# Three modulation vectors on TensorE in column groups, and decay matrices in two interleaved coroutines

## The chip, the cores and the metric

One core of a Trainium2 chip runs the whole program. The metric is device time in microseconds (us), from the first instruction to the last; small is good.

## The reference, cut to what matters

Two transformer blocks run over a sequence of 256 tokens of width 1024, all in float32. The first block is modulated by a condition `c`: eight vectors of 1024 numbers come out of one row times a matrix each.

```python
c_act = jax.nn.silu(c)                                   # (1, 1024)
mod = c_act @ w_ada[l] + b_ada[l]                        # w_ada: 1024 x 6144
sh1, sc1, g1, sh2, sc2, g2 = jnp.split(mod, 6, axis=-1)  # six vectors of 1024
h = modulate(rms_norm(x, norm1_w[l]), sh1, sc1)
mix = hybrid_mixer(h, ...)      # h @ w_in, gated delta rule over 8 heads, short convolution
x = x + g1[:, None, :] * mix
h = modulate(rms_norm(x, norm2_w[l]), sh2, sc2)
x = x + g2[:, None, :] * swiglu(h, ...)
shf, scf = jnp.split(c_act @ w_ada_f + b_ada_f, 2, axis=-1)
```

Inside the mixer each of the 8 heads has a log-decay `g` per token; `decay[c, s] = exp(g_c - g_s)` for `c >= s`, a triangular matrix per head and half of the sequence, weighs the products `k k^T` and `q k^T`. A triangular inverse of `I + beta * (k k^T) * decay` then gives what the heads write. The second block (attention with a position bias, a convolutional FFN) is not touched.

## The kernel before, in words

Activations lie transposed, features on the 128 partitions, 256 tokens along the free axis. A **unit** is one 128-wide column block of a weight matrix times all 256 tokens. Float32 accuracy is had by splitting each weight tile into two float32r halves: ScalarE copies `raw` to `whi`, VectorE subtracts to get `wlo`, and TensorE runs three 128x256 matmuls per 128 rows of the contraction (`whi` times high, `whi` times low, `wlo` times high activations), 24 for a unit of 1024 rows. They write to four PSUM banks `mm0` to `mm3`. Everything else that TensorE does (transposes, the heads' small float32 products) goes to four banks `sd0` to `sd3`.

Weights come in **chunks** of up to 1 MB through a ring of four `raw` buffers (RAW = 4), issued by SyncE in a fixed order. A buffer is given back when its last reader is through. Splits are made up to four units ahead (LAG = 4).

The order of the work is not written out: the program text runs a planner. Coroutines (`gens`) hold the side work (decays, keys, inverses), `postq` the work on a finished unit's PSUM bank; each has an estimated ready time, and `tick()` steps those whose time has come between two triples of matmuls. `account()` holds the planner's prices. What comes out is one fixed order per engine, and each engine works in that order. When the planner has nothing to put in, `pump()` moves its clock on and the engines simply wait.

What the change touches:

- `ada_chunk(v, j)`: one 1 MB chunk holds rows 256j to 256j+255 of the 1024 columns of vector `v`. Three of the vectors, G1, SC2 and SH2, are needed only at the output projection (`post_wo`); their 12 chunks are sprinkled among the units from the short-convolution stage to the projection. VectorE multiplies a 128x1024 half chunk by its column of `cact` and adds it to `acc` (8 operations per vector), and `ada_finish` then transposes `acc` in eight 128x128 pieces on TensorE and sums over the free axis with two reductions.
- `gdn_gates`: makes the gates, then the decay matrices `gD[:, h]` of the 8 heads one after the other: ScalarE scales two masks (`gx`), TensorE makes three products (`sd<-ce,gx` and `sd<-cn,gsums`), ScalarE takes the exponential, GpSimd masks it.
- `gdn_k(h)`: the product `k k^T` of a head (`sd<-KQ`), its norms, and the decayed matrix `AK`. It waits for the key `"D"`, which stands for all 8 heads.
- `small_inverses`: when all 8 `AK` are there, they go through DRAM into another layout, VectorE does a back-substitution of 31 steps (`ct<-KQ,KQ` and `KQ<-KQ,ct`), and the result returns through DRAM (`blk<-KQ`, then `U<-blk`) to be transposed on TensorE (`sd<-cn,U`) by `inverse`.
- `post_z(j)`: the first gate unit takes the buffer that the masks `ce` lie in (tag K).

Of the kernel before, what the change touches and what calls it, by code (L numbers as in the profile page):

```python
# [11 lines left out]
F32 = mybir.dt.float32  # L12
# [32 lines left out]
BK = 32  # L45

C_ID, C_LV = 0, 128
C_GT = C_LV + len(LEVELS) * P
C_LE = C_GT + P
C_ALL = C_LE + P  # L50

# [1 line left out]
def shape_constants():  # L53
    t = np.arange(P)
    c = np.zeros((P, C_ALL), np.float32)
    c[:, C_ID:C_ID + P] = np.eye(P)
    c[:, C_GT:C_GT + P] = 1.0 * (t[:, None] > t[None, :])
    c[:, C_LE:C_LE + P] = 1.0 * (t[:, None] <= t[None, :])
    for i, b in enumerate(LEVELS):
        o = C_LV + i * P  # L60
        c[:, o:o + P] = 1.0 * (((t[:, None] // b) % 2 == 1) & ((t[None, :] // b) == (t[:, None] // b) - 1))
    dist = np.arange(255, -1, -1)
    nf = np.maximum(dist, 1).astype(np.float32)
    large = 16 + (np.log(nf / np.float32(16)) / np.float32(math.log(128 / 16)) * np.float32(16)).astype(np.int32)
    bucket = np.where(dist < 16, dist, np.minimum(large, 31))
    onehot = (bucket[None, ::-1] == np.arange(32)[:, None]).astype(np.float32)
    return c, onehot
# [3 lines left out]
def body(ctx, tc, a, out):  # L71
# [19 lines left out]
    def front():  # L91
        return max(now[0], et["PE"])
# [51 lines left out]
    def timed(fn, dep):  # L144
        save = dict(cur)
        cur.update(dep=dep, end=dep, eng=None, n=0)
        fn()
        r = cur["end"], cur["n"]
        cur.update(save)
        return r  # L150
# [111 lines left out]
    def bank():  # L262
        i = freeb.popleft()
        return i, pss.tile([P, 512], F32, name=f"sd{i}", tag=f"sd{i}", bufs=1)
# [33 lines left out]
    colC = cst.tile([P, P], F32, name="colC")  # L298
    colD = cst.tile([P, P], F32, name="colD")
    cact = cst.tile([P, KT], F32, name="cact")  # L300
    mod = cst.tile([P, 8, KT], F32, name="mod")
    a1 = cst.tile([P, KT], F32, name="a1")
    a2 = cst.tile([P, KT], F32, name="a2")
# [50 lines left out]
    def emit_event():  # L354
        kind, ci, e = events[st["ev"]]
        load_chunks(ci + 1)
        while st["load"] <= ci:
            t, fn = dq.popleft()
            timed(fn, t)
        raw = chunks[ci]["v"]  # L360
        st["ev"] += 1
        last = st["ev"] == len(events) or events[st["ev"]][1] != ci
        if kind == "w":
            u = e
            n, w = u["nk"], u["ncols"]
            hi = splp.tile([P, KT, P], F32R, name="whi", tag="whi")
            lo = splp.tile([P, KT, P], F32R, name="wlo", tag="wlo")
            if not u["tok"]:
                r = raw[:, :, u["off"]:u["off"] + w]
            else:  # L370
                r = raw[:, u["off"]:u["off"] + n]
                hi, lo = (v.rearrange("p (k a) c -> p k (a c)", a=KT // 2) for v in (hi, lo))
            t, _ = timed(lambda: A.activation(hi[:, :n, :w], r, AF.Copy), chunks[ci]["t"])
            u["hi"], u["lo"] = hi, lo

            def low():
                u["rdy"], _ = timed(lambda: V.tensor_tensor(lo[:, :n, :w], r, hi[:, :n, :w].bitcast(F32), OP.subtract), t)
                if last:
                    chunks[ci]["free"] = u["rdy"]
                    load_chunks(len(chunks))  # L380
            lows.append((t, low, u["idx"]))
        else:
            dq.append((chunks[ci]["t"], lambda: e(raw, 0)))

            def second():
                e(raw, 1)
                if last:
                    chunks[ci]["free"] = et["V"]
                    load_chunks(len(chunks))
            dq.append((chunks[ci]["t"], second))  # L390
# [11 lines left out]
    def acc_tile(v):  # L402
        if v == G2:
            accs_["t"] = slot.tile([P, D], F32, name="acc", tag="E")
        return accs_["t"]

    def ada_chunk(v, j):
        src = a["w_ada"][0] if v < 6 else a["w_ada_f"]
        ci = chunk(src, 2 * j, 2, (v if v < 6 else v - 6) * D, D)

        def go(raw, i):
            k = 2 * j + i
            if k == 0:
                if "ada" in state:
                    wait_gens(("mod", state["ada"]))
                state["ada"] = v
                acc = acc_tile(v)
                V.tensor_scalar(acc, raw[:, 0, :], cact[:, 0:1], None, op0=OP.mult)
            else:
                acc = accs_["t"]  # L420
                V.scalar_tensor_tensor(acc, raw[:, i, :], cact[:, k:k + 1], acc, op0=OP.mult, op1=OP.add)
            if k == KT - 1:
                start(ada_finish(v), 9)
        ada_event(ci, go)

    def ada_finish(v):
        acc = accs_["t"]
        for m0 in (0, 4):
            while not len(freeb):
                yield 0  # L430
            i, b = bank()
            for m in range(4):
                PE.transpose(b[:, m * P:(m + 1) * P], acc[:, (m0 + m) * P:(m0 + m + 1) * P], ident)
            yield 1
            V.tensor_reduce(mod[:, v, m0:m0 + 4], b.rearrange("p (m c) -> p m c", c=P), axis=AX.X, op=OP.add)
            freeb.append(i)
        yield 1
        V.tensor_tensor(mod[:, v], mod[:, v], colA[:, v * 8:v * 8 + 8], OP.add)
        if v == SC1:
            V.scalar_tensor_tensor(a1, mod[:, SC1], 1.0, colA[:, 64:72], op0=OP.add, op1=OP.mult)  # L440
        elif v == SC2:
            V.scalar_tensor_tensor(a2, mod[:, SC2], 1.0, colA[:, 72:80], op0=OP.add, op1=OP.mult)
        elif v == SHF:
            V.tensor_tensor(sha, mod[:, SHF], colA[:, 88:96], OP.mult)
        elif v == SCF:
            V.scalar_tensor_tensor(cf, mod[:, SCF], 1.0, colA[:, 80:88], op0=OP.add, op1=OP.mult)
            V.tensor_tensor(cfa, cf, colA[:, 88:96], OP.mult)
        done.add(("mod", v))
        yield
# [75 lines left out]
    def gdn_gates(t):  # L525
# [43 lines left out]
        sums = cst.tile([P, 2, GH], F32, name="gsums")  # L569
        V.tensor_copy(sums.rearrange("p j c -> p (j c)"), b[:, 0:2 * GH])  # L570
        freeb.append(i)
        for h in range(GH):
            yield from space("gx")
            while not len(freeb):
                yield 0
            i, b = bank()
            t = take("gx")
            g2 = t.rearrange("p (t c) -> p t c", c=P)
            for t_ in range(2):
                A.activation(g2[:, t_], gt, AF.Copy, scale=gg[:, t_, h:h + 1])  # L580
            yield
            PE.matmul(b[:, 0:P], g2[:, 0], le, start=True, stop=True)
            PE.transpose(b[:, P:2 * P], sums[:, 1, h:h + 1].to_broadcast([P, P]), ident)
            PE.matmul(b[:, 2 * P:3 * P], g2[:, 1], le, start=True, stop=True)
            give(t)
            yield
            b3, d3 = (v.rearrange("p (k c) -> p k c", c=P)[:, 0:3:2] for v in (b[:, 0:384], gD[:, h]))
            A.activation(d3, b3, AF.Exp)
            A.activation(gD[:, h, P:2 * P], b[:, P:2 * P], AF.Exp, bias=sums[:, 0, h:h + 1])
            freeb.append(i)  # L590
            yield
            G.tensor_tensor(d3, d3, le[:, None, :].to_broadcast([P, 2, P]), OP.mult)
            yield
        done.add("D")


    ctiles, sct = {}, {}
# [118 lines left out]
    def post_z(j):  # L716
        def f(ps, rel):
            if j == 0:
                zg["z"] = slot.tile([P, KT, S], F32, name="zT", tag="K")
            A.activation(zg["z"][:, j], ps[:, :S], AF.Silu)  # L720
            rel()
            done.add(("z", j))
            yield
        return f
# [21 lines left out]
        V.scalar_tensor_tensor(second, b[:, 256:384], wsc[:, h, 1:2], gD[:, h, 256:384], op0=OP.mult, op1=OP.mult)  # L746

    def gdn_k(h):
        while not len(freeb) or "D" not in done:
            yield 0  # L750
        if "AK" not in state:
            state["AK"] = slot.tile([P, 3, GH, P], F32, name="AK", tag="AK")
# [352 lines left out]

    def post_wo(j):
        def f(ps, rel):
            V.scalar_tensor_tensor(xT[:, j], ps[:, :S], mod[:, G1, j:j + 1], xT[:, j], op0=OP.mult, op1=OP.add)
            rel()
            if j == 0:  # L1110
                next_alloc(h2, "h2h", "h2l", "HI", W2)
                ext_cols(h2["h"], mod[:, SH2])
            yield
            yield from next_input(h2, (j,), a2, "h2")
            if j == KT - 1:
                start(rms_rows(rows2, "rms2"), 3)
                start(normed(h2n, ("L", "AK"), "rms2", "h2n", a2, rows2, mod[:, SH2]))
        return f
# [110 lines left out]
    def post_ffn_out(j0):  # L1229
        def f(ps, rel):  # L1230
            if j0 == 0:
                next_alloc(xa, "xah", "xal", "HI", W2)
                ext_cols(xa["h"], sha)
            for o in range(2):
# [411 lines left out]
    V.tensor_copy(colA[:, 64:72], b[:, 64:72])  # L1646
    freeb.append(i)
    A.activation(cact, colA[:, 104:112], AF.Silu)

    accs_["t"] = slot.tile([P, D], F32, name="acc", tag="E")  # L1650
    ac4 = accs_["t"].rearrange("p (b v c) -> p b v c", v=2, c=P)
# [328 lines left out]
```

## Time and profile before

| | before |
|---|---|
| time, median of 3 runs | 880.76 us (879.03 to 881.55) |
| profiled execution, its own time | 880.34 us |
| its span, first to last instruction | 878.6 us |
| mean granted TensorE clock | 0.99 |
| TensorE busy / VectorE busy | 843.0 us (96%) / 695.6 us (79%) |
| ScalarE busy / GpSimd busy | 498.6 us (57%) / 70.6 us (8%) |

Busy shares are means over stages. A busy TensorE here means that matmuls overlap without a gap: one 128x256 matmul is shown with about 0.28 us, but the next starts about 0.115 us after it, so the pitch from start to start and not the shown duration is the cost of one. PE is TensorE, DVE VectorE, ACT ScalarE, POOL GpSimd, SPq the queue in which SyncE issues transfers. Nearly every operation stands under one line, that of the helper `call`, so the rows are told apart by tile names.

### The profile page before, as it was taken

To read this page: it belongs to the slowest core of one execution; us is meant where nothing else is said; L and a number is where in the kernel's file an instruction comes from. 1 tells how busy PE (TensorE), PEld (TensorE's weight loads), DVE (VectorE), ACT (ScalarE), POOL (GpSimd) and SP (SyncE) were. 2 spreads that over 40 slices of the span, in tenths; PEclk is the share of its full clock that TensorE was granted. 3 is DMA by queue.
4 is the path that set the end of the run, shared out by engine and by line. 5 is a ranking of instruction groups with operands and counts; after the bars stand their busy time and mean duration, and the time that the engine had idled before them with its cause. 6 is when DMAs were issued, how large, how long until landed. Compare 5 with 4: busy or idle time off the path is not lost.

```text
span 878.6 us, 17104 instructions
## 1 busy us (share of the span) xinstructions
PE 843.0 (96%) x6847; PEld 815.1 (93%) x6847; DVE 695.6 (79%) x1314; ACT 498.6 (57%) x902; POOL 70.6 (8%) x83
## 2 busy tenths in 40 slices
PE   6999999997999999999999999999999989999995
PEld 6999899997999999999999999998889989999884
DVE  5899998799858889989877555788758888988452
ACT  3359664455656655575455443567666746777341
POOL 3100023000001200200000011200004000000000
PEclk9999999999999999999999999999999989999998
DMA  9995892656814787758988585652435365555521
GB/s 293 309 300 182 271 300 97 168 193 188 267 61 149 229 281 244 253 180 286 339 284 289 171 276 180 197 188 97 135 107 179 112 214 193 191 171 192 193 71 48
DMA packets 158063, 177.35 MB, mean 202 GB/s; under 512 B 9052, under 2 KB 143584, under 8 KB 157984
## 3 DMA queue, kind: packets, MB, share of 16 engines
q1 hardware_dynamic: 156000, 172.57, 60.7%
q0 software_dynamic: 1472, 3.06, 1.1%
q8 instruction: 54, 0.88, 0.4%
q10 hardware_dynamic: 512, 0.62, 0.2%
q14 instruction: 25, 0.20, 0.1%
HBM read 174.64 MB, written 1.60 MB: 201 GB/s over the span
## 4 chain that ended last, share of the span: by engine, by line
PE 57%; issue 21%; DVE 12%; ACT 6%; DMA 2%; SPq 1%; POOL 1%; POOLq 0%; ACTq 0%; DVEq 0%
PE mm L136 49%; PE sd L136 9%; DVE wlo L136 4%; ACT whi L136 2%; DVE cv L136 2%; DVE acc L136 1%; DMA xtok<-in_x_dram 1%; DMA raw<-in_w_in_dram 1%; SPq L136 1%; DVE ct L136 1%; DMA U<-blk 1%; DVE sct L136 0%; ACT L136 0%; DMA blk<-KQ 0%; ACT KQ L136 0%
## 5 line engine op out<-in xcount | busy, mean ns | idle before, releaser
L136 DVE TENSOR_TENSOR wlo<-raw,whi 128x1024 fp32r<-128x1024 f32 (+2 forms) x267 | 320.1, 1206 | 84.2 <-ACT whi L136 81.0
L136 ACT ACTIVATE whi<-raw 128x1024 fp32r<-128x1024 f32 (+2 forms) x267 | 273.5, 1033 | 145.8 <-PE mm L136 122.7
L136 PE MATMUL mm<-h1h,whi 128*128 128x256 f32 x552 | 160.1, 293 | 0.5 <-ACT h1h L136 0.4
L136 PE MATMUL mm<-h1h,wlo 128*128 128x256 f32 x552 | 153.7, 281 | 2.5 <-DVE wlo L136 2.5
L136 PE MATMUL mm<-h1l,whi 128*128 128x256 f32 x552 | 154.1, 281 | 0.5 <-DVE h1l L136 0.3
L136 PEld LDWEIGHTS mm<-h1h,wlo 128*128 128x128 f32 x552 | 103.9, 189 | 3.1 <-DVE wlo L136 2.9
L136 PEld LDWEIGHTS mm<-h1h,whi 128*128 128x128 f32 x552 | 104.5, 191 | 1.8 <-ACT h1h L136 1.2
L136 PEld LDWEIGHTS mm<-h1l,whi 128*128 128x128 f32 x552 | 103.9, 189 | 1.4 <-DVE h1l L136 1.2
L136 PE MATMUL mm<-ynh,whi 128*128 128x256 f32 x288 | 81.7, 284 | 4.2 <-DVE gx L136 4.2
L136 PE MATMUL mm<-h2nh,wlo 128*128 128x256 f32 x288 | 80.1, 278 | 1.9 <-DVE wlo L136 1.9
L136 PE MATMUL mm<-ynl,whi 128*128 128x256 f32 x288 | 81.1, 282 | 0.0
L136 PE MATMUL mm<-ynh,wlo 128*128 128x256 f32 x288 | 81.1, 281 | 0.0
L136 PE MATMUL mm<-h2nh,whi 128*128 128x256 f32 x288 | 80.4, 279 | 0.0
L136 PE MATMUL mm<-h2nl,whi 128*128 128x256 f32 x288 | 80.0, 278 | 0.0
L136 DVE SCALAR_TENSOR_TENSOR acc<-raw,cact,acc 128x1024 f32<-128x1024 f32 (+1 forms) x78 | 71.3, 914 | 1.6 <-DMA raw<-in_w_ada_f_dram 0.2
L136 PEld LDWEIGHTS mm<-ynh,whi 128*128 128x128 f32 x288 | 55.7, 193 | 4.3 <-issue 4.3
L136 PE MATMUL mm<-xah,whi 128*128 128x258 f32 x192 | 57.2, 298 | 0.0
L136 PEld LDWEIGHTS mm<-h2nh,wlo 128*128 128x128 f32 x288 | 54.1, 188 | 2.1 <-DVE wlo L136 2.1
L136 PEld LDWEIGHTS mm<-ynl,whi 128*128 128x128 f32 x288 | 55.5, 193 | 0.0
L136 PEld LDWEIGHTS mm<-ynh,wlo 128*128 128x128 f32 x288 | 55.4, 192 | 0.0
L136 PEld LDWEIGHTS mm<-h2nl,whi 128*128 128x128 f32 x288 | 54.5, 189 | 0.0
L136 PE MATMUL mm<-xal,whi 128*128 128x256 f32 x192 | 54.4, 283 | 0.0
(335 smaller groups left out, 2108.3 us busy)
## 6 DMA issues: line engine op xcount, KB each, us to landing
raw<-in_w_in_dram SPq DMA_DIRECT2D x30, 1024.0 KB, 5.3
raw<-in_w_ffn_in_dram SPq DMA_DIRECT2D x22, 1024.0 KB, 7.0
raw<-in_w_up_dram SPq DMA_DIRECT2D x22, 1024.0 KB, 5.1
raw<-in_w_ada_dram SPq DMA_DIRECT2D x16, 1024.0 KB, 5.3
raw<-in_w_qkv_dram SPq DMA_DIRECT2D x12, 1024.0 KB, 5.2
raw<-in_w_down_dram SPq DMA_DIRECT2D x10, 1024.0 KB, 5.0
raw<-in_w_ada_dram SPq DMA_DIRECT2D x16, 512.0 KB, 7.0
raw<-in_w_o_dram SPq DMA_DIRECT2D x8, 1024.0 KB, 5.9
```

What stands on the lines that cost most here:

```text
L136: r = fn(*args, **kw)
```

## The change

For G1, SC2 and SH2 the sums over the contraction move to TensorE. `cact32` holds each column of `cact` 32 times; with it as a stationary operand of 32 columns a matmul writes only 32 PSUM partitions, and the four products of a chunk (two row halves by two halves of 512 columns) go to the four partition groups 0, 32, 64 and 96 of one bank. The bank is copied (first chunk, ScalarE) or added (the other three, VectorE) to a 128x512 accumulator, and at the end eight matmuls with one moving column, a selector of two partitions, give the vector in columns. The chunk's `raw` buffer is now given back by TensorE. G2, SHF and SCF keep the old way.

The decay matrices are made by two coroutines, one with the even heads and one with the odd, a key waits for its own head's decay only, and `post_z(0)` waits for all eight before it takes the buffer of the masks.

```diff
+    cact32 = cst.tile([P, KT, 32], F32, name="cact32")
...
         while st["load"] <= ci:
-            t, fn = dq.popleft()
-            timed(fn, t)
+            if dq:
+                t, fn = dq.popleft()
+                timed(fn, t)
+            elif not tick_gens():
+                now[0] = front() + 0.1
+        if kind == "p":
+            st["ev"] += 1
+            gens.append(dict(gen=e(), t=chunks[ci]["t"] + 1.0, back=BACK))
+            return
...
+    def ada_rows(ci, v, j):
+        while ("adar", v) in state and state["adar", v] != j or not len(freeb):
+            yield 0
+        raw = chunks[ci]["v"]
+        i, b = bank()
+        t0 = et["PE"]
+        for k in range(2):
+            for h in range(2):
+                g = 32 * (2 * k + h)
+                PE.matmul(b[g:g + 32, :], cact32[:, 2 * j + k], raw[:, k, h * 512:(h + 1) * 512], start=True, stop=True)
+        et["PE"] -= (et["PE"] - t0) * 0.75
+        chunks[ci]["free"] = et["PE"] + 0.3
+        load_chunks(len(chunks))
+        yield 1
+        acc = accs_["t"][:, (v == SC2) * 512:(v == SC2) * 512 + 512]
+        if j == 0:
+            A.activation(acc, b, AF.Copy)
+        else:
+            V.tensor_tensor(acc, acc, b, OP.add)
+        freeb.append(i)
+        state["adar", v] = j + 1
+        if j < 3:
+            return
+        yield 1
+        yield from get()
+        i, b = bank()
+        for m in range(KT):
+            PE.matmul(b[:, m:m + 1], acc[:, m % 4 * P:(m % 4 + 1) * P], cn[:, C_SEL + m // 4:C_SEL + m // 4 + 1],
+                      start=True, stop=True)
+        yield 1
+        V.tensor_tensor(mod[:, v], b[:, 0:KT], colA[:, v * 8:v * 8 + 8], OP.add)
...
     def ada_chunk(v, j):
+        if v in (G1, SC2, SH2):
+            state["ada"] = SH2
+            ci = chunk(a["w_ada"][0], 2 * j, 2, v * D, D)
+            events.append(("p", ci, lambda: ada_rows(ci, v, j)))
+            return
...
-        for h in range(GH):
+        for r in range(2):
+            start(gdn_decays(range(r, GH, 2), sums, gt, le), 6)
+
+    def gdn_decays(hs, sums, gt, le):
+        for h in hs:
             yield from space("gx")
...
             G.tensor_tensor(d3, d3, le[:, None, :].to_broadcast([P, 2, P]), OP.mult)
-            yield
-        done.add("D")
+            done.add(("D", h))
+            yield
...
     def post_z(j):
         def f(ps, rel):
             if j == 0:
+                while any(("D", h) not in done for h in range(GH)):
+                    yield
                 zg["z"] = slot.tile([P, KT, S], F32, name="zT", tag="K")
+            while "z" not in zg:
+                yield
...
     def gdn_k(h):
-        while not len(freeb) or "D" not in done:
+        while not len(freeb) or ("D", h) not in done:
             yield 0
...
+    A.activation(cact32, cact[:, :, None].to_broadcast([P, KT, 32]), AF.Copy)
```

The planner's order shifts with it. On TensorE, late in the value units: `sd<-cn,gx` are the transposes of the heads' values, `sd<-cn,U` those of the first inverse group, `mm<-h1h,whi` and its like the large matmuls. Before, the order there was:

```order
L136 MATMUL sd_2754<-cn,gx_2626 128x128 x2
L136 MATMUL mm_2727<-h1h,whi 128x256
L136 MATMUL mm_2727<-h1l,whi 128x256
L136 MATMUL mm_2727<-h1h,wlo 128x256
L136 MATMUL sd_2778<-cn,gx_2661 128x128 x2
L136 MATMUL sd_2794<-cn,gx_2696 128x128 x2
L136 MATMUL sd_2800<-cn,U 128x128 x4
L136 MATMUL sd_2805<-cn,U 128x128 x4
```

and now, around the same transposes of `U`:

```order
L139 MATMUL mm_2710<-h1h,whi 128x256
L139 MATMUL mm_2710<-h1l,whi 128x256
L139 MATMUL mm_2710<-h1h,wlo 128x256
L139 MATMUL sd_2751<-cn,U 128x128 x4
L139 MATMUL sd_2756<-cn,U 128x128 x4
L139 MATMUL mm_2710<-h1h,whi 128x256
L139 MATMUL mm_2710<-h1l,whi 128x256
L139 MATMUL mm_2710<-h1h,wlo 128x256
L139 MATMUL sd_2765<-cn,gx_2714 128x128 x2
```

The transposes of `U` stood behind the last transposes of the values, after 1320 large matmuls on the `mm` banks, with nothing between; now they stand after 1263 of them, inside a unit.

On VectorE, where the short convolution (`sct`) runs and the sum of G1 begins, the order before was:

```order
L136 COPY gsums<-sd_1240 128x16
L136 TENSOR_SCALAR acc<-raw,cact 128x1024
L136 SCALAR_TENSOR_TENSOR acc<-raw,cact,acc 128x1024 x2
L136 TENSOR_TENSOR gx_1302<-mm_1262,ct_1229 128x256
L136 SCALAR_TENSOR_TENSOR sct<-gx_1204,colB,sct 128x255
L136 SCALAR_TENSOR_TENSOR sct<-gx_1204,colB,sct 128x254
L136 SCALAR_TENSOR_TENSOR acc<-raw,cact,acc 128x1024
L136 TENSOR_TENSOR wlo<-raw,whi 128x1024
```

and now:

```order
L139 TENSOR_TENSOR acc<-acc,sd_1210 128x512
L139 COPY gsums<-sd_1262 128x16
L139 TENSOR_TENSOR wlo<-raw,whi 128x1024
L139 SCALAR_TENSOR_TENSOR sct<-gx_1221,colB,sct 128x255
L139 SCALAR_TENSOR_TENSOR sct<-gx_1221,colB,sct 128x254
L139 TENSOR_TENSOR acc<-acc,sd_1281 128x512
L139 TENSOR_TENSOR wlo<-raw,whi 128x1024
L139 TENSOR_TENSOR gx_1355<-mm_1299,ct_1254 128x256
```

The 1024-wide multiply-adds from `raw` are gone from the queue, 512-wide additions out of PSUM stand in their place, and the weight subtraction `wlo` follows sooner. Further down, the eight `AK` products come between the 33rd and the 38th `wlo` of the program instead of the 41st and the 44th, and the back-substitution ends behind the 56th instead of the 60th. From the first projection units (`mix`) on, the order on VectorE is the same as before.

## Rows read from the trace of the kernel before

**Rows 1.** The page: busy time of the engines, share of the span, instructions.
```profile
PE 843.0 (96%) x6847; PEld 815.1 (93%) x6847; DVE 695.6 (79%) x1314; ACT 498.6 (57%) x902; POOL 70.6 (8%) x83
```

**Rows 2.** Stretches: length, busy us of each engine, granted clock, DMA share, GB/s.
```profile
80.00:340.00 260.00, 251.31 (x2135) 247.20 (x2134) 225.51 (x445) 153.35 (x291) 27.09 (x25) 0.99 0.61 195
...
200.00:222.00 22.00, 17.24 (x132) 16.58 (x131) 21.13 (x43) 12.75 (x29) 0.00 (x0) 0.92 0.61 182
...
218.50:221.80 3.30, 3.07 (x15) 3.10 (x16) 3.26 (x5) 2.05 (x5) 0.00 (x0) 0.50 0.88 302
```

**Rows 3.** Timeline of TensorE at its waits: start, us, operation [idle before <-releaser].
```profile
103.66 0.39 PE L136 MATMUL mm<-h1h,wlo 128*128 128x256 f32 x1 [1.68 <-DVE wlo L136]
...
110.12 0.49 PE L136 MATMUL sd<-ce,gx 128*128 128x128 f32 x2 [0.75 <-ACT gx L136]
...
208.26 0.38 PE L136 MATMUL mm<-h1h,wlo 128*128 128x256 f32 x1 [0.83 <-DVE wlo L136]
...
216.22 0.44 PE L136 MATMUL sd<-cn,gx 128*128 128x128 f32 x2 [1.86 <-ACT gx L136]
218.73 1.94 PE L136 MATMUL sd<-cn,U 128*128 128x128 f32 x8 [2.07 <-DMA U<-blk]
...
293.93 0.63 PE L136 MATMUL sd<-cn,ot 128*128 128x128 f32 x4 [0.73 <-DVE ot L136]
...
347.34 0.39 PE L136 MATMUL mm<-mixl,whi 128*128 128x256 f32 x1 [0.81 <-DVE mixl L136]
...
393.71 0.39 PE L136 MATMUL mm<-h2nh,wlo 128*128 128x256 f32 x1 [1.89 <-DVE wlo L136]
```

**Rows 4.** The chain that ended last, 205 to 223 us: start, us, what.
```profile
207.09 2.96 DMA blk<-KQ
...
213.82 4.78 DMA U<-blk
```

**Rows 5.** Timeline of TensorE where attention uses two column groups of 64.
```profile
607.23 0.28 PE L136 MATMUL mm<-xah,wlo 128*128 128x258 f32 x1
607.43 0.44 PE L136 MATMUL sd<-oatp,oats 128*64 128x256 f32 x2
...
608.24 0.38 PE L136 MATMUL mm<-xah,whi 128*128 128x258 f32 x1
608.46 0.28 PE L136 MATMUL mm<-xal,whi 128*128 128x256 f32 x1
```

**Rows 6.** Timeline of TensorE: float32 products, one-column products, transposes of `acc`.
```profile
282.09 0.81 PE L136 MATMUL sd<-KQ 128*128 128x256 f32 x4
282.74 0.50 PE L136 MATMUL sd<-ones,sq 128*128 128x1 f32 x4
...
54.12 0.94 PE L136 MATMUL sd<-cact,raw 128*128 128x1 f32 x8
54.92 0.36 PE L136 MATMUL mm<-h1h,whi 128*128 128x256 f32 x1
...
119.55 0.60 PE L136 MATMUL sd<-cn,acc 128*128 128x128 f32 x4
119.91 0.37 PE L136 MATMUL mm<-h1h,whi 128*128 128x256 f32 x1
```

**Rows 7.** A group of VectorE operations, 80 to 330 us: count | busy us, mean ns.
```profile
L136 DVE SCALAR_TENSOR_TENSOR acc<-raw,cact,acc 128x1024 f32<-128x1024 f32 x21 | 27.0, 1287 | 0.2
```

**Rows 8.** The chain that ended last: long runs of matmuls, start, us, count.
```profile
145.57 40.99 PE mm L136 x348
...
431.37 43.20 PE mm L136 x381
```

**Rows 9.** Groups of GpSimd operations, 80 to 330 us.
```profile
L136 POOL TENSOR_TENSOR gD<-gD,ce 128x256 f32<-128x256 f32 x8 | 7.8, 979 | 98.2 <-ACT gD L136 98.2
...
L136 POOL TENSOR_TENSOR rk<-ssk,nhalf 128x2 f32<-128x2 f32 x8 | 6.5, 817 | 9.3 <-DVE ssk L136 9.1
```

**Rows 10.** The page, DMA issues: KB each, us from issue to landing.
```profile
raw<-in_w_ada_dram SPq DMA_DIRECT2D x16, 1024.0 KB, 5.3
```

More of the change, by code (lines that the diff above doesn't have):

```diff
@@ L47 @@
 C_ID, C_LV = 0, 128
-C_GT = C_LV + len(LEVELS) * P
+C_SEL = C_LV + len(LEVELS) * P
+C_GT = C_SEL + 2
 C_LE = C_GT + P
@@ L61, in shape_constants @@
         c[:, o:o + P] = 1.0 * (((t[:, None] // b) % 2 == 1) & ((t[None, :] // b) == (t[:, None] // b) - 1))
+    for i in range(4):
+        c[32 * i, C_SEL + i % 2] = 1.0
     dist = np.arange(255, -1, -1)
@@ L405, in acc_tile, with have @@
         return accs_["t"]
-    def ada_chunk(v, j):
+    def ada_rows(ci, v, j):
[29 more added lines that the diff above has]
+        V.tensor_tensor(mod[:, v], b[:, 0:KT], colA[:, v * 8:v * 8 + 8], OP.add)
+        freeb.append(i)
+        if v == SC2:
+            V.scalar_tensor_tensor(a2, mod[:, SC2], 1.0, colA[:, 72:80], op0=OP.add, op1=OP.mult)
+        done.add(("mod", v))
+    def have(*vs):
+        while any(("mod", v) not in done for v in vs):
+            yield 0
+    def ada_chunk(v, j):
+        if v in (G1, SC2, SH2):
[3 more added lines that the diff above has]
+            return
         src = a["w_ada"][0] if v < 6 else a["w_ada_f"]
@@ L440, in ada_finish @@
             V.scalar_tensor_tensor(a1, mod[:, SC1], 1.0, colA[:, 64:72], op0=OP.add, op1=OP.mult)
-        elif v == SC2:
-            V.scalar_tensor_tensor(a2, mod[:, SC2], 1.0, colA[:, 72:80], op0=OP.add, op1=OP.mult)
         elif v == SHF:
@@ L571, in gdn_gates @@
         freeb.append(i)
-        for h in range(GH):
+        for r in range(2):
+            start(gdn_decays(range(r, GH, 2), sums, gt, le), 6)
+    def gdn_decays(hs, sums, gt, le):
+        for h in hs:
             yield from space("gx")
-            while not len(freeb):
-                yield 0
+            yield from get()
             i, b = bank()
@@ L1107, in f @@
         def f(ps, rel):
+            if j == 0:
+                yield from have(G1, SC2, SH2)
             V.scalar_tensor_tensor(xT[:, j], ps[:, :S], mod[:, G1, j:j + 1], xT[:, j], op0=OP.mult, op1=OP.add)
@@ L1231, in f @@
             if j0 == 0:
+                yield from have(G2, SHF, SCF)
                 next_alloc(xa, "xah", "xal", "HI", W2)
```

## The prediction

> **What bounds the kernel now.** I read the page first: TensorE is busy 96% of the span [rows 1]. A busy share says little for overlapping matmuls, so the stretches and the timeline come next. From 80 to 340 us, where the change works, TensorE is busy 251.3 of 260 us and VectorE 225.5 [rows 2]. TensorE runs its queue in a fixed order and almost without a pause; the reader should see there that any work put into this queue moves the end, and that the most that can be won back is the pauses. So the third view is the timeline at TensorE's waits [rows 3]. In and just behind the stretch the large ones are: 1.68 us at 103.66 and 0.83 at 208.26 for a `wlo`, 1.86 at 216.22 for a value head from ScalarE, 2.07 at 218.73 for the transfer of `U`, 0.73 at 293.93 and 0.81 at 347.34 for VectorE; 0.75 at 110.12 for the decays' `gx`; and 1.89 at 393.71, in a part whose order does not change. One loss is no pause: from 218.5 to 221.8 us the granted clock is 0.50, 1.2 instead of 2.4 GHz, right behind the two long pauses [rows 2]. 3.3 us at half the clock lose 1.65.
>
> The chain that ended last says what holds TensorE at 218.73: the back-substitution ends, the block goes out at 207.09 (2.96 us) and comes back at 213.82 (4.78 us) [rows 4].
>
> **What the change adds to TensorE.** First the price of a float32 product on the whole array: the two of a head, 256 and 128 columns, take from 282.09 to 282.74, 0.65 us for 384 columns [rows 6], so 512 columns take 0.87 us. Four of them one after another would be 3.47 us for a chunk.
>
> The change puts them into four column groups. The trace has groups of 64 in attention: four products (256, 256, 128 and 128 columns), two in each group. Two products have started and been shown to their end within 0.44 us, so the groups do run side by side [rows 5]. The whole insertion costs 608.46 - 607.23 = 1.23 us less the two pitches of 0.12 us that the large matmuls around it would take anyway, 0.99 us. 384 columns per group, side by side, are 0.65 us by the price above; the other 0.34 us is getting in and out. I take the same for four groups: 0.87 + 0.34 = **1.21 us a chunk**, 14.5 us for 12 chunks. No row shows four groups at once. The bounds: 0.87 us (no cost of getting in and out), 10.4 us in all; 3 x 0.87 more (no overlap), 3.81 us a chunk and 45.7 in all. I stay near the lower one because the two groups of rows 5 overlap fully.
>
> The Trainium skill's page "TensorE: Matmul & The Clock Gate", section "Measured speedup vs the span model", has three column groups of 32 columns with 512 moving columns at 2.38 times the speed of one after another, 79% of the ideal three. An estimate from that page for four groups is 3.47 / (4 x 0.79) = 1.09 us a chunk, which would make the sum 1.4 us smaller; the two groups of rows 5 have 1.30 / 0.99 = 1.3 of the ideal two, because their products are short.
>
> The finish of a vector changes from eight transposes to eight products with one moving column. Four one-column float32 products take from 54.12 to 54.92, 0.80 us; four transposes of `acc` take from 119.55 to 119.91, 0.36 us [rows 6]; the first large matmul behind an insertion takes 608.46 - 608.24 = 0.22 instead of 0.12 us [rows 5]. One insertion of 1.60 + 0.10 replaces two of 0.36 + 0.10: +0.78 us a vector, and I take 2.4 us in all. Bounds: with 0.36 us for two products, as 282.74 and its four passes show [rows 6], it is 1.9 instead of 2.4; nothing nearer is to be had.
>
> The Trainium skill's page "TensorEngine Tiling (Array Packing)", section "Instruction Overhead", puts a matmul with one moving column at about 60 cycles; at 2.4 GHz that is an estimate of 0.03 us, and the 24 products would cost 4 us less than the rows give. The trace disagrees: 0.20 us each, with a 128-column weight load for each of two passes.
>
> Together TensorE gets **+16.9 us**. The copy that fills `cact32` is one ScalarE operation in the start, where ScalarE waits for the input tokens; I take nothing for it, and 0.3 us if that cover is gone (256 columns, a quarter of the width of the operation in rows 7). The decay products are the same ones in other places: nothing.
>
> **What it takes from VectorE.** 21 multiply-adds go, 27.0 us, with three first multiplications and six reductions beside them; nine additions of half that width come, some 0.64 us each by the same row [rows 7], 5.8 us. VectorE is some 25 us lighter between 80 and 340 us, but this counts only where TensorE waits for it.
>
> **What TensorE gets back.** A pause costs its idle time and about 0.16 us more, since the last matmul is shown with 0.28 us where its pitch is 0.12.
> - 103.66: `wlo` was queued behind multiply-adds of G1 and a late `whi`; in the new order the subtractions stand ahead. 1.84 us.
> - 208.26, 216.22 and 218.73, and the half clock behind them: keys no longer wait for the last decay, so the eight `AK` and the back-substitution come sooner. It ends four subtractions sooner (56th instead of 60th); four units of 24 matmuls at 0.1178 us (40.99 us for 348 [rows 8]) are 11.3 us. The transposes of `U` stand 57 matmuls sooner, 6.7 us, but TensorE also carries seven chunks more by then, 8.5 us. Without the pauses TensorE would have come to `U` 1.86 + 2.07 = 3.9 us sooner, so that much the block was late; it gains 11.3 - 6.7 + 8.5 = 13. Nothing is late there next, so 0.99 + 2.02 + 2.23 + 1.65 = 6.9 us come back.
> - 293.93 and 347.34: VectorE arrives late by less than a microsecond, and it is lighter by 20 us or more there: 0.89 + 0.97 = 1.9 us.
>
> The wait for `gx` at 110.12 and one like it stay, since the decays still go through ScalarE, and so does 393.71. Together **-10.6 us**.
>
> The sum: 16.9 - 10.6 = +6.3 us. The profiled execution took 880.34 us, 0.4 us less than the median of the three runs, so I forecast **886.6 us**. Changes under 0.3% (2.6 us) cannot be told from none here.
>
> **Rivals.**
> 1. *New waits.* The decays come in pairs, and keys right behind them. GpSimd has 8 x (0.979 + 0.817) = 14.4 us of masks and powers [rows 9], formerly in two rounds, now in one of about 141 large matmuls, 16 us; VectorE's `AK` waits for them in order, with the weight subtractions queued behind it and TensorE behind those. TensorE itself now waits for the chunk's landing, 5.3 us after issue [rows 10]. Four more waits as at 110.12, 0.91 us each, give +3.6: 890. For it: VectorE had no slack around 100 us. Against: four units are split ahead. Chance 0.17.
> 2. *Groups only two at a time.* Then a chunk costs 2 x 0.87 + 0.34 = 2.08 us and the time is 886.6 + 10.4 = 897. Chance 0.07. None at once: 3.81 us, +31, 918. Chance 0.05. Against both: rows 5.
> 3. *Not slower: the pitch.* Large matmuls run at 0.1178 us in one long run and at 0.1134 in another with the same operands' shapes (43.20 us for 381 [rows 8]). A run keeps its value until something else is inserted; what sets it the rows do not say. Between 80 and 340 us there are 70 units, 1,680 matmuls; all of them fast instead of half of them would give 1,680 / 2 x 0.0044 = 3.7 us: 882.9, within 0.3%. It decides from there: 3.6 us are needed. Chance 0.15. The same could go the other way inside the range.
> 4. *Faster.* The insertion costs nothing for getting in and out (-4.1) and the pitch turns too: 878.8 or less with the `gx` waits gone as well. Nothing in the rows speaks for it. Chance 0.08.
>
> **How the numbers follow.** My forecast, 884 to 889.5 us, has 0.48. With rival 1 (to 894) and rival 3 (from 880) it makes 0.80: the range is 880 to 894 us. Slower: 0.48 + 0.17 + 0.12 = 0.77, less a little of my own case at its lower edge, 0.76; within 0.3%: 0.16; faster: 0.08.
>
> **What would show it.** Right: a chunk's four products start within some hundredths of a microsecond of each other, and TensorE's next large matmul follows 1.2 us after the one before the insertion; the transposes of `U` start without a wait; no half clock near 220 us; VectorE's queue idle more often. Wrong: a chunk at 2 or 3.8 us; pauses of TensorE ahead of `sd<-raw,cact` for the landing, or at the decays, beyond 2 us together; or the long runs all at one pitch.

## The result, and the profile after

The changed kernel takes 887.2 us (median of 7 runs, 884.9 to 893.0) against 880.2 for the kernel before (7 runs): ratio 1.0095, interval 1.0070 to 1.0119: slower by about 1%, a small change but clear of noise. The forecast was 886.6. The profiled execution is the longest of the seven, 893.0 us; a second profile of the same kernel (below) has a span of 885.1, and where the two differ I say so.

The page after, span and busy time, against [rows 1]:

```profile
span 891.2 us, 17344 instructions
...
PE 861.6 (97%) x6967; PEld 823.1 (92%) x6967; DVE 670.5 (75%) x1293; ACT 503.3 (56%) x908; POOL 68.1 (8%) x83
```

VectorE lost 25.1 us of work, as forecast, and the time rose all the same: TensorE is busy 97% of the span, and its busy time rose by 18.6.

One chunk in the timeline of TensorE, and the finish of SC2 (start, us, operation, instructions):

```profile
77.58 0.28 PE L139 MATMUL mm<-h1h,wlo 128*128 128x256 f32 x1
77.79 1.06 PE L139 MATMUL sd<-raw,cact 128*32 128x512 f32 x8
78.79 0.38 PE L139 MATMUL mm<-h1h,whi 128*128 128x256 f32 x1
79.01 0.29 PE L139 MATMUL mm<-h1l,whi 128*128 128x256 f32 x1
...
272.56 0.28 PE L139 MATMUL mm<-h1h,wlo 128*128 128x256 f32 x1
272.68 1.84 PE L139 MATMUL sd<-cn,acc 128*128 128x1 f32 x16
274.38 0.36 PE L139 MATMUL mm<-h1h,whi 128*128 128x256 f32 x1
274.58 0.28 PE L139 MATMUL mm<-h1l,whi 128*128 128x256 f32 x1
```

An insertion is read from the start of the large matmul ahead of it to the start of the second one behind it, less two pitches (0.23 us). A chunk: 79.01 - 77.58 - 0.23 = 1.20 us. A finish: 274.58 - 272.56 - 0.23 = 1.79.

What TensorE waited for from 70 to 420 us (total, times, longest), the three longest after, then the first of them in the second profile:

```profile
PE sd L139 <- DMA U<-blk: 2.3, 1, 2.3
PE mm L139 <- DVE wlo L139: 2.1, 2, 1.9
PE mm L139 <- DVE mixl L139: 0.4, 1, 0.4
```
```profile
PE sd L139 <- DMA U<-blk: 2.0, 1, 2.0
```

Against [rows 3]: the waits at 103.66, 208.26, 216.22 and 293.93 are gone, those for `gx` at 110.12 and 122 too, the one for `mixl` has halved, the 1.9 us for `wlo` at 393.71 stands. The wait for `U`, which the forecast counted as won, is still there.

Why, SyncE's queue says. Its issues around the block's way (start, us):

```profile
196.69 0.95 SPq L139 DMA_DIRECT2D blk<-KQ  x1
200.42 0.37 SPq L333 DMA_DIRECT2D raw<-in_w_ada_dram  x1
200.88 7.96 SPq L333 DMA_DIRECT2D raw<-in_w_in_dram  x2
209.02 3.37 SPq L139 DMA_DIRECT2D U<-blk  x4
```

And what that queue waited for in the same stretch, and how the way back ended (the chain):

```profile
SPq L333 <- DVE wlo L139: 7.1, 1, 7.1
```
```profile
211.38 4.58 DMA U<-blk
```

The block goes out at 196.69, 10.4 us sooner than in [rows 4]. But the four transfers of its return are issued only at 209.02: ahead of them stand three loads of weights, and the last of these waits 7.1 us for a buffer that VectorE's subtraction still reads. In the kernel before, way out to landing took 213.82 + 4.78 - 207.09 = 11.5 us; now it takes 211.38 + 4.58 - 196.69 = 19.3. Of the 10.4 us won, 7.8 were lost in the queue and on the way. The traffic around the way out is another, too: before, from the issue to the landing, and after, five microseconds from the issue on (columns as in [rows 2], the last two are the DMA share and GB/s):

```profile
207.09:210.05 2.96, 2.13 (x18) 1.92 (x18) 2.92 (x4) 0.99 (x3) 0.00 (x0) 1.00 0.57 119
```
```profile
196.70:201.70 5.00, 5.00 (x44) 3.99 (x43) 3.89 (x5) 3.10 (x8) 0.00 (x0) 1.00 1.06 357
```

The stretch behind the wait (length, busy us of PE, PEld, DVE, ACT and POOL, granted clock, DMA share, GB/s):

```profile
217.30:222.30 5.00, 5.00 (x32) 5.00 (x31) 1.16 (x2) 1.59 (x5) 0.00 (x0) 0.66 0.77 246
```

TensorE has just paused 2.3 us, and the clock is again granted at half for a part of the stretch, 5.00 x 0.34 = 1.7 us lost, as much as behind the pauses of [rows 2].

### The profile page after: what moved, and what is told of

It reads as the page before. It is cut to its first block, busy times and chain, and to the rows that moved or that the text cites. A ratio compares the mean times of both kernels' runs of the same rounds, so it can differ in the third digit from the quotient of the medians.

```text
span 891.2 us, 17344 instructions
## 1 busy us (share of the span) xinstructions
PE 861.6 (97%) x6967; PEld 823.1 (92%) x6967; DVE 670.5 (75%) x1293; ACT 503.3 (56%) x908; POOL 68.1 (8%) x83
## 4 chain that ended last, share of the span: by engine, by line
PE 54%; issue 20%; DVE 5%; ACT 3%; DMA 2%; SPq 0%; POOL 0%; POOLq 0%; ACTq 0%; DVEq 0%
PE mm L139 47%; PE sd L139 8%; DVE wlo L139 2%; ACT whi L139 1%; DMA KQ<-blk 1%; DVE ct L139 1%; DVE cv L139 1%; DMA U<-blk 1%; SPq L139 0%; DMA blk<-AK 0%; DVE ynt L139 0%; DVE KQ L139 0%; ACT oats L139 0%; DVE acc L139 0%; ACT h2nt L139 0%
## 5 line engine op out<-in xcount | busy, mean ns | idle before, releaser
L139 PEld LDWEIGHTS mm<-h1h,whi 128*128 128x128 f32 x552 | 104.5, 190 | 11.5 <-issue 10.1
L139 PEld LDWEIGHTS mm<-h2nh,whi 128*128 128x128 f32 x288 | 54.9, 191 | 0.0
```

Source lines behind the costliest of these rows:

```text
L139: r = fn(*args, **kw)
```

## The experiments

All were timed in three batches, each on a chip of its own together with the kernel before (medians there 879.0, 880.0 and 880.4 us): first `sums_only`, `decays_only`, `chunk_twice` and `after_again`; then `u_first`, `fin2`, `g1_only` and `g1_ufirst_fin2`; then the other four. Runs of different batches are therefore compared by their ratios. Theory after the comparison: the sums cost TensorE what was forecast; what is given back depends on who is late around 100 us and on the way of the block. Rivals: the decays and keys cost, not the sums; or the sums cost another price.

**The two halves apart: `sums_only`, `decays_only`, and the whole again, `after_again`.** `sums_only` is the changed kernel with the old decays, the key `"D"` and the old `post_z`:

```diff
-        for r in range(2):
-            start(gdn_decays(range(r, GH, 2), sums, gt, le), 6)
...
-        for h in hs:
+        for h in range(GH):
             yield from space("gx")
...
-            done.add(("D", h))
-            yield
+            yield
+        done.add("D")
...
-        while not len(freeb) or ("D", h) not in done:
+        while not len(freeb) or "D" not in done:
```

`decays_only` is the opposite edit in the kernel before. `after_again` is the changed kernel untouched.

> The three vectors summed by TensorE, with the decays, the keys' wait and the order of the masks as in the kernel before. Theory (the sums are the price, the keys' new wait brings something back): TensorE gets 12 x 1.20 + 3 x 0.9 = 17.1 us, the pauses that VectorE made come back (103.66, 293.93, 347.34: some 3.7 us), the others stay; 880.2 + 13.4 = 893.6, between 890 and 897, slower than the changed kernel (887.2). Rival (the interleaved decays cost, and VectorE's relief pays most of the sums): 887 or less.

> The kernel before with the decays in two interleaved coroutines and the keys' wait per head, the three vectors still summed on VectorE. Theory: nothing is added to TensorE; the keys and the back-substitution come sooner, but VectorE still holds the 27 us of multiply-adds and TensorE's waits for wlo stay; 880.2 less 0 to 4 us: 876 to 881. Rival (the decays in pairs bring new waits of TensorE for gx and of VectorE for GpSimd's masks): 883 to 888, and waits for gx of more than 3.1 us together.

> The changed kernel once more, unchanged: a second profile of it. Theory: 887.2 within 3 us; its wait of TensorE for the transfer of U near 217 us is there again, 2 to 3 us, because SyncE's queue has the block's four return transfers behind loads that wait for buffers; the waits for the last decays stay below 1 us together. Rival (that wait is chance of the one profile): no wait above 0.5 us for U.

Measured: `sums_only` 891.4 us, 1.0131 (1.0101 to 1.0161); `decays_only` 880.6, 1.0017 (0.9990 to 1.0043); `after_again` 886.4, 1.0077 (1.0049 to 1.0106). The price lies in the sums. The new decays alone change nothing that can be told, but not because nothing happens. TensorE's waits in `decays_only`, 70 to 350 us:

```profile
PE sd L136 <- DVE mod L136: 4.5, 1, 4.5
PE sd L136 <- DVE AK L136: 2.0, 1, 2.0
PE mm L136 <- DVE wlo L136: 1.1, 1, 1.1
```

and VectorE there, with the reduction of G1 (`mod`), which gives the bank free, queued behind subtractions and `AK`:

```profile
129.96 0.74 DVE L136 SCALAR_TENSOR_TENSOR AK<-sd,wsc,gD 128x256 f32<-128x256 f32 x2
130.62 2.35 DVE L136 TENSOR_TENSOR wlo<-raw,whi 128x1024 fp32r<-128x1024 f32 x2
...
133.96 2.35 DVE L136 TENSOR_TENSOR wlo<-raw,whi 128x1024 fp32r<-128x1024 f32 x2
136.22 0.68 DVE L136 TENSOR_REDUCE mod<-sd 128x4 f32<-128x512 f32 x1
```

The waits for `gx` and `U` are all but gone there, and 6.5 us of others on VectorE have come. The granted clock is at half around the longest of them:

```profile
131.00:141.00 10.00, 5.51 (x24) 4.82 (x23) 9.79 (x25) 0.95 (x3) 0.70 (x1) 0.51 0.74 255
```

TensorE is busy 5.5 of these 10 us, so an estimated 5.51 x 0.49 = 2.7 us more go there. In `sums_only` TensorE waits 5.3 us for `cv` (VectorE's convolution, at 221.56 and 234.06); the last steps of the back-substitution, late as before, stand in VectorE's timeline between the two, at 227 us. `after_again` shows the 2.0 us wait for `U` again, so it is no accident of one execution.

**The price of a chunk: `chunk_twice`.** The order of everything else on each engine is the same, because the planner's clock (`et`) is set back.

```diff
+        t1 = et["PE"]
+        for k in range(2):
+            for h in range(2):
+                g = 32 * (2 * k + h)
+                nc.tensor.matmul(b[g:g + 32, :], cact32[:, 2 * j + k], raw[:, k, h * 512:(h + 1) * 512], start=True, stop=True)
+        et["PE"] = t1
```

> The changed kernel with each chunk's four products issued twice in a row into the same bank; the order of everything else on each engine is the same. Theory (a chunk is 0.87 us of columns in four groups side by side and 0.34 us of getting in and out, and TensorE has no slack): the second set costs the columns alone, 12 x 0.87 = 10.4 us: 897.6, between 895 and 900. If it pays the whole price again: 12 x 1.20 = 14.4, 901.6. If half of it falls into pauses that TensorE has anyway: 892.

Measured: 895.6 us, 1.0171 (1.0144 to 1.0197), 9.2 above `after_again`. One chunk, and the wait for `U`:

```profile
77.75 0.28 PE L139 MATMUL mm<-h1h,wlo 128*128 128x256 f32 x1
77.96 1.07 PE L139 MATMUL sd<-raw,cact 128*32 128x512 f32 x8
78.84 1.04 PE L434 MATMUL sd<-raw,cact 128*32 128x512 f32 x8
79.81 0.39 PE L139 MATMUL mm<-h1h,whi 128*128 128x256 f32 x1
80.03 0.28 PE L139 MATMUL mm<-h1l,whi 128*128 128x256 f32 x1
```
```profile
PE sd L139 <- DMA U<-blk: 0.5, 1, 0.5
```

The insertion is 80.03 - 77.75 - 0.23 = 2.05 us: the second set costs 0.85, the columns alone, and getting in and out costs 0.35 once. 12 x 0.85 = 10.2; of this TensorE takes 1.5 out of the wait for `U`, which it now reaches later (2.0 to 0.5): 8.7, against 9.2 measured. So a wait that the trace names does absorb work put ahead of it. That the sum comes so close is partly chance: `after_again` has half clock for 1.7 us of loss each behind G1's finish and at its wait for `U`, and the profile of `chunk_twice` has neither. Around its own wait for `U`, at 218.50, the granted clock is 1.00:

```profile
214.00:224.00 10.00, 9.52 (x82) 7.78 (x82) 4.76 (x8) 5.32 (x11) 0.00 (x0) 1.00 1.02 296
```

**The finish: `fin2`.** Both selector columns in one product, four products a vector instead of eight. The planner answers with another order on all engines from about 119 to 318 us, so that the time holds more than the price of the finish.

```diff
-        for m in range(KT):
-            PE.matmul(b[:, m:m + 1], acc[:, m % 4 * P:(m % 4 + 1) * P], cn[:, C_SEL + m // 4:C_SEL + m // 4 + 1],
-                      start=True, stop=True)
+        for m in range(4):
+            PE.matmul(b[:, 2 * m:2 * m + 2], acc[:, m * P:(m + 1) * P], cn[:, C_SEL:C_SEL + 2], start=True, stop=True)
...
```

> The changed kernel with the finish of a vector made of four products with two moving columns instead of eight with one. Theory (such a product costs 0.20 us by its weight load and two passes, not by its columns): the finishing insertion falls from 1.79 to 1.0 us, three times, 2.4 us: 884.3, between 883 and 886. Rival (the price goes by columns): the insertion stays at 1.8 us and the time at 886.7.

Measured: 881.0 us, 1.0020 (1.0003 to 1.0037), below its range; the gain is 0.57% or 5.0 us against `after_again`, where 2.4 were forecast. The insertion:

```profile
265.13 0.28 PE L139 MATMUL mm<-h1h,wlo 128*128 128x256 f32 x1
265.25 0.95 PE L139 MATMUL sd<-cn,acc 128*128 128x2 f32 x8
266.06 0.36 PE L139 MATMUL mm<-h1h,whi 128*128 128x256 f32 x1
266.26 0.28 PE L139 MATMUL mm<-h1l,whi 128*128 128x256 f32 x1
```

266.26 - 265.13 - 0.23 = 0.90 instead of 1.79: the price goes by passes and not by columns, and the three make 2.7 us. That is half of the 5.0 us. The rest is not shown piece by piece. The wait for `U` fell from 2.0 to 1.1 us in its profile, and the clock behind G1's finish is another, in `after_again` and in `fin2`:

```profile
118.00:128.00 10.00, 9.76 (x68) 9.48 (x68) 8.13 (x32) 5.67 (x14) 4.22 (x6) 0.83 0.35 110
```
```profile
118.00:128.00 10.00, 9.82 (x79) 9.52 (x80) 8.33 (x34) 5.79 (x15) 4.61 (x6) 1.00 0.24 82
```

10.00 x 0.17 = 1.7 us. Both profiles of the changed kernel have 0.83 there, right behind 1.6 us in which TensorE ran one-column products only; but `u_first`, `u_pool`, `g1_only` and `g1_upool` below have the same finish and 1.00. So the finish does not decide it alone, and what does stays open.

**The way back of the block: `u_first` and `u_pool`.** The first issues no load between the block's way out and its way back (`hold`, true from the one to the other); with it the planner also shifts the order on TensorE from 209 to 256 us. The second leaves the order on TensorE, VectorE and ScalarE as it is and issues the return on GpSimd's queue.

```diff
-        while st["load"] < min(upto, len(chunks)):
+        while st["load"] < min(upto, len(chunks)) and not st.get("hold"):
...
+        st["hold"] = True
...
+        st["hold"] = False
+        load_chunks(len(chunks))
```
```diff
-            SY.dma_start(UV[m * BK:(m + 1) * BK, :, m * BK:(m + 1) * BK], s2[:, m].rearrange("g s t -> s g t"))
+            dst = UV[m * BK:(m + 1) * BK, :, m * BK:(m + 1) * BK]
+            nc.gpsimd.dma_start(dst, s2[:, m].rearrange("g s t -> s g t"))
+            account("SY", "dma_start", (dst,), {})
```

> The changed kernel, with no weight load issued on SyncE's queue between the block's way out and its way back, so that the four transfers into U stand right behind it. Theory (U is late because its four issues stand behind three loads, one of which waits 7.1 us for a buffer): TensorE's wait for U (2.0 to 2.3 us) goes, with 0.16 us of emptying and some 0.5 us of half clock; 886.7 - 2.8 = 883.9, between 882.5 and 885.5. Rival (the way back itself takes that long, or the loads now behind it come late): the wait for U stays above 1.5 us, or as much appears ahead of mm for whi or wlo: 886 or more.

> The changed kernel with the four transfers into U issued on GpSimd's queue instead of SyncE's; the order on TensorE, VectorE and ScalarE is the same, instruction by instruction. Theory (they are late by their place in SyncE's queue): TensorE's wait for U (2.0 to 2.3 us) goes; 886.7 - 2.5 = 884.2, between 882.5 and 885.7. Rival (the block's way is slow whatever the queue): the wait stays above 1.2 us, 886 or more.

Measured: `u_first` 884.6 us, 1.0053 (1.0029 to 1.0076); `u_pool` 882.1, 1.0027 (1.0007 to 1.0048). Neither profile has a wait for `U`, nor a half clock in that place. In `u_pool` the block goes out, and GpSimd waits for it and issues:

```profile
194.54 0.90 SPq L139 DMA_DIRECT2D blk<-KQ  x1
```
```profile
202.57 2.67 POOL L916 DMA_DIRECT2D U<-blk  x4 [26.29 <-DMA blk<-KQ]
```
```profile
211.36 1.06 PE L139 MATMUL sd<-cn,U 128*128 128x128 f32 x8 [0.26 <-DVE wlo L139]
```

This splits the lateness. With no load ahead of the return, 202.57 - 194.54 = 8.0 us still pass from the one issue to the other in `u_pool`, and 201.49 - 194.19 = 7.3 in `u_first`, where [rows 4] has 2.96 for the way out. In the changed kernel 209.02 - 196.69 = 12.3 passed. So, as an estimate, 4 to 5 us were the place in the queue and another 4 to 5 the longer way out. That way is longer where more is moved: 2.96 us at a DMA share of 0.57 before, 5.54 at 0.83 in `g1_upool` below, and, up to the issue of the return, 7.3 at 0.95 in `u_first` and 8.0 at 1.06 in `u_pool`. No run changed the traffic alone, so that it is the cause is not shown.

`u_first` gained 0.24% against `after_again`, 2.1 us, but the intervals overlap, so that this gain is not shown by the time, only the loss of the wait by the profile. `u_pool` gained 0.50%, 4.4 us, more than the 2.5 expected and just below its range; its profile also lacks the half clock of the stretch above, 1.7 us.

**Only G1 on TensorE: `g1_only`, and the same with the old decays, `sums_g1`.**

```diff
-        if v in (G1, SC2, SH2):
-            state["ada"] = SH2
+        if v in (G1,):
+            state["ada"] = v
...
```

> The changed kernel with only G1 summed by TensorE; SC2 and SH2 are summed by VectorE as in the kernel before. Theory (only the stretch from 80 to 120 us had a VectorE without slack, so only G1's relief brings something back): TensorE loses 8 x 1.20 + 2 x 0.9 = 11.4 us, and the small waits at 293.93 and 347.34 return, 1.5 us: 886.7 - 9.9 = 876.8, between 874 and 880, 2 us below the kernel before. Rival (the relief counts in every stretch, so taking it back makes new waits of TensorE for VectorE): 883 or more.

> Only G1 summed by TensorE, with the decays and the keys' wait as in the kernel before. Theory (the two halves of the change need each other: the relief of VectorE around 100 us is what lets earlier keys come through): TensorE gets 4 x 1.20 + 0.9 = 5.7 us and gets back 103.66 alone, 1.8 us: 879.5 + 3.9 = 883.4, between 881 and 887. Rival (G1's relief alone brings g1_only's gain): 877 or less.

Measured: `g1_only` 874.8 us, 0.9942 (0.9920 to 0.9963), faster than both kernels; `sums_g1` 886.8, 1.0070 (1.0043 to 1.0096). The stretch from 200 to 240 us in `g1_only` and in `sums_g1`:

```profile
200.00:240.00 40.00, 38.82 (x349) 38.16 (x348) 30.58 (x48) 23.32 (x47) 1.12 (x1) 1.00 0.74 224
```
```profile
200.00:240.00 40.00, 29.88 (x231) 28.54 (x230) 36.79 (x67) 24.09 (x42) 0.00 (x0) 0.91 0.66 202
```

With the old keys the back-substitution stands in VectorE's timeline until 220.28 us, and TensorE is busy 29.9 of 40 us at a granted clock of 0.91; with the new keys it is through before 200 us, and TensorE is busy 38.8 at the full clock.

Side by side, as ratios to the kernel before:

| summed by TensorE | old decays | new decays |
|---|---|---|
| none | 1 | 1.0017 |
| G1 | 1.0070 | 0.9942 |
| G1, SC2, SH2 | 1.0131 | 1.0077 |

The new decays are worth nothing alone, 1.3% (11 us) beside G1, 0.5% beside all three. From G1 to all three with the new decays is 1.35%, 11.9 us, and TensorE's added work is 8 x 1.20 + 2 x (1.79 - 0.90) = 11.4: relieving VectorE of SC2 and SH2 brought nothing back that can be told.

**Still better? `g1_fin2`, `g1_upool`, `g1_ufirst_fin2`.** The edits above on top of `g1_only`.

> Only G1 summed by TensorE, finished by four products with two moving columns. Theory: the one finish falls from 1.79 to 0.90 us as in fin2, 874.8 - 0.9 = 873.9, between 872 and 876. Rival (the small shift sets another order further on, which costs more than it brings): 877 or more.

> Only G1 summed by TensorE, and the four transfers into U on GpSimd's queue; the order on TensorE, VectorE and ScalarE is that of g1_only. Theory: g1_only's wait for U (1.2 us) goes, 874.8 - 1.3 = 873.5, between 872 and 875.5. Rival (as much traffic in the same time, so that the loads of the next weights land later): a wait of 1 us or more for whi, wlo or gx between 205 and 225 us, 875 or more.

> Only G1 by TensorE, the way back of U right behind its way out, and the finish with two-column products. Theory: g1_only's 876.8 less 2.8 for U and 0.8 for one finish: 873.2, between 871 and 877, faster than both kernels. Rival (with VectorE loaded again, U is late for another reason, the back-substitution): as g1_only, less 1 us at most.

Measured: 876.9 us, 0.9964 (0.9941 to 0.9987); 875.8, 0.9951 (0.9930 to 0.9973); 879.7, 0.9993 (0.9967 to 1.0018). None beats `g1_only` (874.8, 0.9942); the first two can't be told from it, since the intervals overlap. All three lie above their ranges, by 0.9, 0.3 and 2.7 us, and the third is 6.5 us above its forecast. Its profile has a new wait of TensorE, and ScalarE's behind it:

```profile
215.90 0.44 PE L139 MATMUL sd<-cn,gx 128*128 128x128 f32 x2 [3.30 <-ACT gx L139]
```
```profile
214.49 1.06 ACT L139 ACTIVATE whi<-raw 128x1024 fp32r<-128x1024 f32 x1 [3.18 <-DMA raw<-in_w_in_dram]
215.45 0.40 ACT L139 ACTIVATE gx<-cv 128x256 f32<-128x256 f32 x1
```

A load that stood ahead of the block's return stands behind it now, lands later, and `gx` is queued on ScalarE behind its copy. In `g1_upool` the wait for `U` is still 1.1 us, because the way back itself now takes long; the chain has

```profile
194.80 5.54 DMA blk<-KQ
...
202.36 8.38 DMA U<-blk
```

where [rows 4] has 2.96 and 4.78. There the wait is the way itself, not the queue. In `g1_fin2` a wait of 2.4 us for `ot` on VectorE has come near 300 us: the rival of its expectation, since the order has shifted from about 118 us on, as in `fin2`.

## Why the forecast was right, step by step

- **A chunk, 1.21 us; 14.5 in all.** Measured 1.20, 14.4. The split into 0.87 of columns and 0.34 of getting in and out holds too: 0.85 and 0.35 by `chunk_twice`. The four products run side by side: 0.85 against the 3.47 reckoned for one after another is 4.1 times. What a single chunk lacks (3.47 / 1.20 is 2.9 times) is entry and exit. Rival 2 falls, and with the 0.35 us of getting in and out rival 4. The Trainium skill's page "TensorE: Matmul & The Clock Gate", section "Measured speedup vs the span model", has 79% of the ideal for three groups; the trace has 2.9 of 4 for a chunk by itself and no loss in a second set behind the first, and the estimate from that page, 1.09 us, is 0.11 below what was measured.
- **The finish, +0.78 a vector.** One insertion of 1.79 (1.70 forecast) replaces two of 0.45: +0.89 a vector, 2.7 in all. By `fin2` four products of two columns make an insertion of 0.90, so one costs some 0.2 us as well. The Trainium skill's page "TensorEngine Tiling (Array Packing)", section "Instruction Overhead", has about 60 cycles for so narrow a product; the trace disagrees, here as before.
- **103.66, 208.26 and 216.22 come back.** Right, 1.84 + 0.99 + 2.02. 293.93 came back, 347.34 by half.
- **218.73 and the half clock come back (2.23 + 1.65).** Wrong. The block did go out 10.4 us sooner (11.3 forecast). The step that failed is "Nothing is late there next, so 0.99 + 2.02 + 2.23 + 1.65 = 6.9 us come back": I moved the block's way out without moving its return past what stands in SyncE's queue, and took its duration from a way out at a DMA share of 0.57. Four issues behind loads, and a way out of an estimated 7 to 8 us instead of 3, ate 7.8 of the 10.4.
- **The waits for `gx` stay (0.75 and 0.51).** Wrong the other way: both are gone, with the emptying 0.75 + 0.51 + 2 x 0.16 = 1.6 us. This hides part of the miss.
- **Net +6.3.** Measured +7.0 at the medians, +7.5 in the second comparison. The terms as measured are 14.4 + 2.7 for TensorE's work, less 10.6 - 3.9 - 0.4 + 1.6 = 7.9 given back, plus 1.7 for the new half clock behind G1's finish: +10.9. The place of 347.34 in [rows 3], where the stretch of the change ends, stands 10.9 us later in the profile after and 8.6 in the second one:

```profile
358.25 0.38 PE L139 MATMUL mm<-mixl,whi 128*128 128x256 f32 x1 [0.40 <-DVE mixl L139]
```
```profile
355.98 0.38 PE L139 MATMUL mm<-mixl,whi 128*128 128x256 f32 x1 [0.40 <-DVE mixl L139]
```

  Of this, 1.1 and 0.9 us stand there already ahead of the first chunk: the transposes `sd<-cn,abT` start at 72.14 before, at 73.24 and 73.00 in these two, but at 71.26 in `u_pool`, so that the copy that fills `cact32` is not what moves them. The stretch itself took 9.8 and 7.8 us more; in the second the fast pitch (rival 3 below) took 1.1 off.

  The spans differ by 891.2 - 878.6 = 12.6 and 885.1 - 878.6 = 6.5. Behind that place, where the order is unchanged, the first profile takes 1.7 us more than the kernel before and the second 2.1 less; pitch and half clock differ there from one execution to the next. So the working was 1.5 to 3.5 us low for the stretch, and that the median came out within 0.6 us of the forecast is partly chance.
- **Rival 1, new waits by the landing or the masks.** Not seen: TensorE has no wait of 0.5 us for either.
- **Rival 3, the pitch.** The two pitches are real, but which one a run gets is no property of the kernel. The long run in the chain, first in the profile after, then in its second profile:

```profile
159.86 31.13 PE mm L139 x262
```
```profile
139.90 49.30 PE mm L139 x435
```

31.13 / 262 is 0.119 us, 49.30 / 435 is 0.113; within, the same 250 matmuls of the same program take 29.3 us in the one and 28.2 in the other. So it widens the spread of the runs, and no row here forecasts it for either kernel.

## What to carry to other kernels

Where an engine works in order and is the bound, work that is moved onto it must be priced against pauses that it really has. Only the part of the move that relieves the late engine pays: here one vector of three did, and only together with the reordering that uses the relief. When a producer is made earlier, follow its result through every queue to the consumer, transfers first, and price the way at the traffic of the new moment, not of the old. Relief and reordering should be tried apart and together; their effects do not add.

## What was not expected of the hardware

The same pause of 1.9 us for `wlo` (at 393.71 in [rows 3]) is followed by the full clock in one profile of the changed kernel and by half clock in the other. The stretch around the pause in the profile after, then in the second one:

```profile
402.00:409.00 7.00, 5.12 (x30) 4.91 (x29) 6.68 (x15) 4.74 (x8) 0.00 (x0) 0.76 0.22 63
```
```profile
399.70:406.70 7.00, 5.12 (x43) 4.91 (x43) 6.71 (x15) 4.77 (x8) 0.00 (x0) 1.00 0.20 68
```

7.00 x 0.24 = 1.7 us hang on that. The seven runs of the changed kernel lie up to 8 us apart. The clock and the pitch are two things seen to differ between them; that they make up the whole spread is not shown. Either is reason enough not to price an effect of 2 us from one profile of each kernel.
